# A two-stream, two-layer network on one core: the instruction order drawn up with the tile context's other machine model

## The chip, the core and the metric

One core of one Trainium2 chip runs the whole program in one launch. The metric is the device time of one execution in microseconds; three timed executions of the kernel before gave 1656.62 us as the median (1654.23 to 1677.01). The core's engines are named as in the profile: PE (matrix products; PEld is its weight load), DVE (vector), ACT (scalar), POOL (GpSimd), and SP, which here only issues DMAs. Each engine has its own queue and takes its instructions strictly in the order in which the program lists them; between engines only semaphores hold the order.

## What is computed

Two streams of 128 tokens (a prompt and a sample) with 1024 channels go through two layers. Cut to what matters:

```python
def trunk_layer(x, mod, lp, ...):
    h = adaln(x, norm_g[0], m[0], m[1]);  x = x + 0.5 * m[2] * swiglu(h, ffn_w_in[0], ffn_w_out[0])
    h = adaln(x, norm_g[1], m[3], m[4]);  x = x + m[5] * token_mixing(h)
    h = adaln(x, norm_g[2], m[6], m[7]);  x = x + 0.5 * m[8] * swiglu(h, ffn_w_in[1], ffn_w_out[1])
...
# token_mixing: RWKV, gated linear attention (GLA), gated delta rule and softmax attention beside each other,
# each times a sigmoid gate and a branch matrix, summed, then w_out
```

`m` holds nine modulation vectors of 1024 values per layer, products of the conditioning vector with `w_mod` (1024 x 9216 per layer). RWKV and the delta rule each solve a triangular system of 128 rows per head, direction and stream.

## The kernel before

The tokens of both streams lie together as 256 columns; every large product has a 128x128 block of weights as the stationary operand and 128x256 activations as the moving one. Weights are float32 in HBM. `wload` (L198) loads a block of up to 128x1024 values into a tile `raw` (three buffers) with a DMA of SP's queue (L206). `split` (L177) turns half of it at a time, 512 columns, into two parts `hi` (ACT, L155) and `lo` (DVE, L158), four buffers each; `gemm` (L219) then makes three products for each 128x128 block, `hi` with both parts of the activations and `lo` with the first. So one `lo` row of 128x512 serves 4 x 3 = 12 products, and one full `raw` block 24. All products are issued in `mm`, L170, and are told apart by the tile that they write: `pg`, `pu` and `po` are the gate, up and output products of a feed-forward part (`ffn`, L460) or the gates, branches and output of the mixing; `pA`, `pB`, `pC`, `pD`, `pR`, `pT` are the mixing's input products.

A modulation vector (`mod_part`, L287) needs eight loads of 128x1024 values into tiles `mraw` (L298; 16 buffers) and eight groups of four products `acc` (L170), 64 records in the profile, then a row copy `modrow` and two transposes `acct`. `queue` and `fill` (L325, L338) write these steps in small portions among the products of a feed-forward part: six vectors in the first, four in the second, four in the third, none in the fourth; the loads and products of the last two vectors of each (`KEEP`) are written to fall into the following norm. One more vector per layer is written into the mixing (`queue_mixing`, L1319).

A norm (`rstd`, L380, and `adaln`, L425) ends a sublayer: squares, products `pss`, a chain of eleven small DVE operations on `nr`, products `prs`, then the normalised activations `hhi` and `hlo`, for which the next large product waits.

In the mixing, `ORDER` (L90) lists the steps of a layer with offsets of priority. Both triangular systems go the same way: `gather` (L806) copies 32x32 diagonal blocks from `SA` (RWKV) or `SD` (delta rule) into `GB`, and sends them to DRAM (`d<-GB`); `inverse` (L824) loads them as `Lb<-d` (L834) and inverts all blocks in 31 steps of two POOL operations each (L842 and L843, tiles `itmp` and `Tb`); `inverse_out` (L847) sends the result to DRAM (`d<-Tb`, L852) and back (`TA<-d`, L855), DVE transposes a half of it into `TB` (L857); `solve` (L860) then makes small products `sv` from it, with ACT and DVE steps between them.

The Python code only lists instructions and priorities. The tile context's scheduler plays the program through on a model of the machine and writes each engine's list in the order in which the instructions went there: an instruction that is ready and has the better priority goes first. In what order the engines' lists stand, SP's and POOL's too, follows from that model.

Of the kernel before, what the change touches and what calls it, by code (L numbers as in the profile page):

```python
# [24 lines left out]
OUT_UNITS = ((0, 2), (2, 2), (4, 2), (6, 1), (7, 1))      # first chunk and number of chunks of the output products  # L25
# [4 lines left out]
# column offsets of w_in  # L30
# [3 lines left out]
def constants():  # L34
    """Tables that depend on shapes alone, packed along the free dimension."""
# [28 lines left out]
    for d in range(2):  # L64
        for l in (16, 8, 4, 2, 1):
            tt = (t16 // l) * 2 * l + t16 % l + (l if d == 0 else 0)      # token of a compact index
            su = (si % (2 * l)) >= l
            ms.append(f((si // (2 * l) == tt // (2 * l)) & (su if d else ~su)))
# [33 lines left out]
class Net:  # L102
    def __init__(self, ctx, tc, ia, oa, dbg=None):
# [13 lines left out]
        self.ch = 0                 # which of the two chains of small products is being written  # L117
# [63 lines left out]
    def after(self, later, earlier):  # L181
        """issue order of two instructions of one queue"""
        self.tc.add_manual_dep(later.ins, earlier.ins.name,
                               mybir.DependencyInfo(mybir.DependencyClass.NoSync, mybir.DependencyReason.DATA),
                               reason="issue order")
# [12 lines left out]
    def wload(self, srcs, nk, nc_):  # L198
        """srcs: list of (column offset in tile, dram view [128, nk, n])."""
# [7 lines left out]
        def part(k0, n):  # L207
            """rows k0 .. k0 + n as two f32r parts that sum to them"""
# [10 lines left out]
    def gemm(self, out2, wview, nkc, xhi, xlo, ncol=256, segs=None):  # L219
        """out2: psum tile [128, 512] -> (2, 256) column chunks; weights  # L220
        stationary, channel-major activations moving."""
# [23 lines left out]
    def params_g(self):  # L245
        """conditioning vectors and modulation biases first, the small parameters later"""
# [40 lines left out]
    def mod_part(self, tiles, l, v):  # L287
        """a modulation vector (1024 columns) as loads and products, a pair per weight tile, and a
        last step. Column groups of 256 in the four column tiles of the PE array."""
# [20 lines left out]
        def last():  # L310
# [5 lines left out]
            # chunk of the vector = j * 2 + c  # L316
# [8 lines left out]
    def queue(self, parts):  # L325
        """modulation work for the rest of the sublayer"""
# [11 lines left out]
    def fill(self, nload, nprod):  # L338
        """the queued loads and products up to these counts, the loads never too few"""
# [5 lines left out]
    def flush(self):  # L345
        """what is left, in the shadow of a norm"""
        if self.mr is not None:
            self.fill(len(self.loads), len(self.prods))
            self.mr.close()
            self.mr = None  # L350

    def modcols(self, l, i):
        """per-sublayer columns: g * (1 + scale), shift, gate factor."""
# [13 lines left out]
    def rsqrt(self, p, n, scale, eps):  # L367
        """(p * scale + eps)^-1/2 of [128, n]: a first guess from the exponent, then three
        Newton steps (the sign alternates)"""
# [10 lines left out]
    def rstd(self):  # L380
        """[128, 256] psum: 1 / rms of every token, on all partitions"""
# [21 lines left out]
    def headnorm(self, x, n, scale, eps):  # L403
        """(sum over each 64-partition group of x^2 * scale + eps)^-1/2: psum tiles of 512 columns of x"""
# [20 lines left out]
    def adaln(self, l, i):  # L425
        """x * g (1 + scale) ahead of the norm factor, which comes last; at the start the
        other way round, as the modulation comes last there"""
# [32 lines left out]
    def ffn(self, l, w, i):  # L460
        """the modulation parts are spread over the products; the last steps (keep) wait for the next norm"""
# [39 lines left out]
    # SBUF of this phase is shared by tag: tiles of one tag have disjoint lives.  # L501
# [29 lines left out]
    def padded(self, p):  # L531
        """[128, (2 chunks, 2 streams, 128)] psum -> sbuf with a zero column at each end"""
# [43 lines left out]
    def proj_gate(self, c0, nm):  # L576
        """x * (1 + tanh(x / 2)): silu without its factor 1/2, which is in the norm weights"""
# [8 lines left out]
    def proj_t(self, l):  # L586
        """token-major: values of B and D, the scalar gates of C"""
# [33 lines left out]
    def proj_d(self, l):  # L621
        """q with the heads in the order 0, 2 | 1, 3, and k"""
# [10 lines left out]
    def rwkv_front(self, l):  # L633
# [10 lines left out]
        S0T = self.t("S0T", [128, 4, 128])       # initial state, transposed, block-diagonal over the heads of a chunk  # L644
# [6 lines left out]
        # decay: sg = 2 sigmoid, log-decay = -RW_C * sg  # L651
# [11 lines left out]
        # in-context rates: ta = 2 a - 1  # L663
# [8 lines left out]
        # normalised keys  # L672
        KR = self.t("c4", [128, 2, 2, 256], name="KR")      # stream, chunk, (kk | r)
# [11 lines left out]
        # token-major values  # L685
# [7 lines left out]
        # output gate  # L693
# [11 lines left out]
        # SA: (stream, dir), (L^T | beta.rho^T), head;  UA: right-hand sides, then solutions  # L705
# [6 lines left out]
        for d in range(2):  # L712
# [22 lines left out]
            BK = self.t("e4", [128, 2, 2, 2, 128], name="BK")       # stream, chunk, (beta | kappa)  # L735
# [11 lines left out]
            for s in range(2):  # L747
                sd = 2 * d + s

                def prod(j, e):  # L750
                    """beta or kappa of the heads e, e + 2 against (alpha | rho)"""
# [32 lines left out]
            # final state operands (context only): beta, kappa decayed to the end, token-major  # L784
# [9 lines left out]
        # bonus  # L794
# [11 lines left out]
    def gather(self, S, d):  # L806
        """32x32 diagonal blocks of the systems of a direction to dram, [s', t] for the
        forward direction, transposed for the backward one"""
# [15 lines left out]
    def inverse(self, S, after):  # L824
        """(I + L)^-1 of all 32x32 diagonal blocks by columns; a block's even columns are on
        one partition, its odd ones on another"""
# [33 lines left out]
    def solve(self, S, U):  # L860
        """in place: U <- (I + L)^-1 U by 32-row blocks, both streams of a direction at once"""
# [29 lines left out]
    def state_out(self, p, dst):  # L891
        """the states are the diagonal 64x64 blocks of the two chunks"""
# [4 lines left out]
    def rwkv_back(self, l):  # L897
# [18 lines left out]
        # group norm over each head  # L916
# [15 lines left out]
    def ymix(self, m, y):  # L932
        """y: [128, chunk, stream, tok] -> parts for the branch products"""
# [8 lines left out]
    def delta_front(self, l):  # L942
# [3 lines left out]
        S0 = self.t("S0", [128, 2, 2, 128], name="S0C")     # dir, chunk: [k of two heads, v], block-diagonal  # L946
        nc.sync.dma_start(out=S0, in_=ia["pk_c"][l].rearrange("p (d c v) -> p d c v", d=2, c=2))
        # l2-normalised q (with the 1/sqrt(dk) factor) and k: KQ [stream, chunk, (k | q)]
        big = self.t("big10", [128, 2560], name="delta")
        KQ = big[:, 0:1024].rearrange("p (s c j t) -> p s c j t", s=2, c=2, j=2)  # L950
        EK = big[:, 1024:2048].rearrange("p (d c j t) -> p d c j t", d=2, c=2, j=2)   # dir, chunk, (k | q)
# [6 lines left out]
        # token-major v, and k of the context  # L958
# [11 lines left out]
        # scalars: beta, log-decay  # L970
# [485 lines left out]
```

## Time and profile before

| | |
|---|---|
| median of three timed executions | 1656.62 us (1654.23 to 1677.01) |
| span of the profiled execution, first to last instruction | 1665.8 us |
| time of the profiled execution around its span | not listed; the span stands for it |
| PE busy | 1620.0 us (97%), 13862 matrix instructions |
| DVE, ACT, POOL busy | 1057.8, 811.3, 143.7 us |
| moved by DMA | 311.14 MB, mean 187 GB/s |

The busy time of an engine is the union of its instructions. A product's record lasts longer than the distance to the next one (they are pipelined), so a busy PE need not be at its fastest; distances between starts tell more. A row's releaser in brackets is what ended the engine's idle time just before it.

### The profile page before, as it was taken

How to read it: one execution, taken by the hardware profiler on the slowest of the kernel's cores; microseconds unless marked ns; L12 is line 12 of the kernel's file. 1: busy time of each engine (PE TensorE's matmuls, PEld its weight loads, DVE VectorE, ACT ScalarE, POOL GpSimd, SP SyncE). 2: the span in 40 equal slices, each digit the busy share in tenths (PEclk: the TensorE clock that was granted, in tenths of full speed). 3: DMA queues.
4: the chain of work that ended last, by engine and by line, in shares of the span. 5: the costliest groups of instructions: out<-in, count | busy, mean ns of one | idle time of the engine just before them, and what ended most of it. 6: DMA issues, size and time to landing. Idle time of an engine off the chain costs nothing.

```text
span 1665.8 us, 34996 instructions
## 1 busy us (share of the span) xinstructions
PE 1620.0 (97%) x13862; PEld 1465.2 (88%) x13872; DVE 1057.8 (64%) x2270; ACT 811.3 (49%) x1529; POOL 143.7 (9%) x304
## 2 busy tenths in 40 slices
PE   6999999999999999999999999999999999999997
PEld 3999988788778998999989999887887899989997
DVE  4555557667687477665566655674857774866655
ACT  3444445446444455454455545551744443655553
POOL 0000000043007000000000000000700350000000
PEclk9999999999999999999999999998989998999999
DMA  9998775344246455976669766551423563645553
GB/s 342 315 318 297 238 238 164 80 117 114 64 132 199 127 173 195 324 266 221 213 228 316 245 213 211 189 139 48 122 74 95 158 195 95 187 143 182 186 184 121
DMA packets 300821, 311.14 MB, mean 187 GB/s; under 512 B 48368, under 2 KB 278768, under 8 KB 300656
## 3 DMA queue, kind: packets, MB, share of 16 engines
q1 hardware_dynamic: 300368, 307.85, 58.2%
q8 instruction: 109, 1.79, 0.4%
q10 hardware_dynamic: 288, 1.05, 0.2%
q14 instruction: 56, 0.46, 0.1%
HBM read 303.87 MB, written 4.98 MB: 185 GB/s over the span
## 4 chain that ended last, share of the span: by engine, by line
PE 75%; DVE 4%; POOL 2%; DMA 2%; ACT 2%; issue 1%; SPq 0%; POOLq 0%; DVEq 0%; ACTq 0%
PE pg L170 20%; PE po L170 15%; PE pu L170 13%; PE wk L170 6%; PE sv L170 4%; PE pA L170 3%; PE acc L170 3%; PE pC L170 1%; PE pD L170 1%; PE yA L170 1%; PE pR L170 1%; PE pT L170 1%; POOL itmp L842 1%; POOL Tb L843 1%; DVE lo L158 1%
## 5 line engine op out<-in xcount | busy, mean ns | idle before, releaser
L158 DVE TENSOR_TENSOR lo<-raw,hi 128x512 fp32r<-128x512 f32 (+2 forms) x840 | 581.0, 696 | 394.0 <-ACT hi L155 381.8
L155 ACT ACTIVATE hi<-raw 128x512 fp32r<-128x512 f32 (+2 forms) x840 | 523.2, 626 | 592.4 <-PE pg L170 192.3
L170 PE MATMUL pg<-hhi,hi 128*128 128x256 f32 x1216 | 356.5, 293 | 6.0 <-ACT hi L155 2.9
L170 PE MATMUL pg<-hlo,hi 128*128 128x256 f32 x1216 | 352.8, 290 | 0.5 <-DVE hlo L158 0.3
L170 PE MATMUL pg<-hhi,lo 128*128 128x256 f32 x1216 | 349.7, 288 | 0.8 <-DVE lo L158 0.6
L170 PEld LDWEIGHTS pg<-hhi,hi 128*128 128x128 f32 x1216 | 236.0, 194 | 23.6 <-issue 8.8
L170 PEld LDWEIGHTS pg<-hlo,hi 128*128 128x128 f32 x1216 | 236.1, 194 | 7.7 <-issue 4.4
L170 PEld LDWEIGHTS pg<-hhi,lo 128*128 128x128 f32 x1216 | 236.7, 195 | 3.1 <-DVE lo L158 2.3
L170 PE MATMUL pu<-hhi,lo 128*128 128x256 f32 x704 | 199.3, 283 | 0.0
L170 PE MATMUL pu<-hlo,hi 128*128 128x256 f32 x704 | 199.2, 283 | 0.0
L170 PE MATMUL pu<-hhi,hi 128*128 128x256 f32 x704 | 199.2, 283 | 0.0
L170 PE MATMUL po<-zhi,hi 128*128 128x256 f32 x704 | 198.6, 282 | 0.0
L170 PE MATMUL po<-zhi,lo 128*128 128x256 f32 x704 | 196.8, 280 | 0.0
L170 PE MATMUL po<-zlo,hi 128*128 128x256 f32 x704 | 196.7, 279 | 0.0
L170 PEld LDWEIGHTS po<-zhi,hi 128*128 128x128 f32 x704 | 132.6, 188 | 6.2 <-issue 4.5
L170 PEld LDWEIGHTS pu<-hhi,lo 128*128 128x128 f32 x704 | 135.2, 192 | 0.1
L170 PEld LDWEIGHTS pu<-hhi,hi 128*128 128x128 f32 x704 | 135.2, 192 | 0.0
L170 PEld LDWEIGHTS pu<-hlo,hi 128*128 128x128 f32 x704 | 135.2, 192 | 0.0
L170 PEld LDWEIGHTS po<-zhi,lo 128*128 128x128 f32 x704 | 132.9, 189 | 0.0
L170 PEld LDWEIGHTS po<-zlo,hi 128*128 128x128 f32 x704 | 132.5, 188 | 0.0
L170 PE MATMUL acc<-mraw,cT 128*32 128x256 f32 x1152 | 85.7, 403 | 9.6 <-DMA mraw<-in_w_mod 9.5
L191 POOL COPY GB<-SA 32x128 f32<-32x128 f32 x16 | 5.7, 355 | 911.2 <-DMA out_o_v<-VD 584.6
(354 smaller groups left out, 2610.6 us busy)
## 6 DMA issues: line engine op xcount, KB each, us to landing
raw<-in_ffn_w_in SPq DMA_DIRECT2D x176, 512.0 KB, 4.5
mraw<-in_w_mod SPq DMA_DIRECT2D x138, 512.0 KB, 5.7
raw<-in_w_in SPq DMA_DIRECT2D x106, 512.0 KB, 3.6
raw<-in_ffn_w_out SPq DMA_DIRECT2D x76, 512.0 KB, 4.4
raw<-in_w_branch SPq DMA_DIRECT2D x32, 256.0 KB, 3.2
raw<-in_w_out SPq DMA_DIRECT2D x16, 512.0 KB, 4.1
raw<-in_ffn_w_out SPq DMA_DIRECT2D x12, 256.0 KB, 3.0
raw<-in_ffn_w_out SPq DMA_DIRECT2D x8, 384.0 KB, 4.4
```

Of the source, the lines that this page charges most:

```text
L155: self.nc.scalar.activation(out, in_, func, bias=bias, scale=scale, **kw)
L158: self.nc.vector.tensor_tensor(out, a, b, op)
L170: self.nc.tensor.matmul(out, lhsT, rhs, start=start, stop=stop)
L191: (self.nc.vector if eng == "v" else self.nc.gpsimd).tensor_copy(out, in_)
L842: nc.gpsimd.tensor_tensor(tv, a, b, ALU.mult)
L843: nc.gpsimd.tensor_tensor(T[:, 0:n, j + 1:32], T[:, 0:n, j + 1:32], tv, ALU.subtract)
```

## The change

The scheduler is told to use its other model of the machine, a simulation of the timeline, when it draws up the order. No instruction is added, removed or altered; matched by name, both programs hold the same 11988 products, 701 DMAs on SP, 2270 DVE and 1508 ACT operations. Waits on semaphores follow the new order. The rest of the diff removes comments.

```diff
-    with _tile.TileContext(nc, pool_alloc_mode="queue") as tc:
+    with _tile.TileContext(nc, pool_alloc_mode="queue", schedule_with_timeline_sim=True) as tc:
         build(tc, ia, oa)
```

First place: SP's queue at the start of the first feed-forward part. Before, from the first three weight blocks on:

```order
L206 DMA raw<-in_ffn_w_in 128x4x256 x3
L298 DMA mraw<-in_w_mod 128x1024 x2
L206 DMA raw<-in_ffn_w_in 128x4x256
L298 DMA mraw<-in_w_mod 128x1024
L253 DMA cst<-in_consts 128x1348
L206 DMA raw<-in_ffn_w_in 128x4x256 x3
L254 DMA wg<-in_constb 128x2688
L206 DMA raw<-in_ffn_w_in 128x4x256
L298 DMA mraw<-in_w_mod 128x1024 x4
L206 DMA raw<-in_ffn_w_in 128x4x256 x3
```

Now, from the same three blocks on:

```order
L206 DMA raw<-in_ffn_w_in 128x4x256 x3
L253 DMA cst<-in_consts 128x1348
L254 DMA wg<-in_constb 128x2688
L298 DMA mraw<-in_w_mod 128x1024 x7
L206 DMA raw<-in_ffn_w_in 128x4x256
L298 DMA mraw<-in_w_mod 128x1024
L206 DMA raw<-in_ffn_w_in 128x4x256
L298 DMA mraw<-in_w_mod 128x1024 x8
L206 DMA raw<-in_ffn_w_in 128x4x256
L298 DMA mraw<-in_w_mod 128x1024 x7
```

This goes on until all 48 `mraw` loads of the six vectors are issued, with 8 weight blocks among them; 33 weight blocks without a modulation load follow. PE's list has moved in the same way: all six vectors' `acc` products stand before the second half of the sixth of 22 `pg` and `pu` groups. In the second feed-forward part the list has the loads of eight vectors, its own four and the four of the third part, 64 `mraw` with 15 weight blocks among them, behind the part's first five blocks and before its last 24 (`ffn_w_in`); their `acc` products stand in the first ten of its 22 groups. The third part has none left.

Second place: PE at the norm after the first feed-forward part. Before:

```order
L170 MATMUL po<-zhi,lo 128x256
L170 MATMUL acc<-mraw,cT 32x256 x8
L170 MATMUL pss<-ones,ssq 128x1 x4
L170 MATMUL pss<-ones,sq 128x1 x2
L170 MATMUL acc<-mraw,cT 32x256 x5
L170 MATMUL pss<-ones,sq 128x1 x2
L170 MATMUL acc<-mraw,cT 32x256 x16
L170 MATMUL prs<-cst,nr 128x128 x2
L170 MATMUL acc<-mraw,cT 32x256 x3
L175 MATMUL acct<-cst,modrow 128x128 x2
L170 MATMUL acc<-mraw,cT 32x256 x32
L170 MATMUL pA<-hhi,hi 128x256
```

Now:

```order
L170 MATMUL po<-zhi,lo 128x256
L170 MATMUL pss<-ones,ssq 128x1 x4
L170 MATMUL pss<-ones,sq 128x1 x4
L170 MATMUL prs<-cst,nr 128x128 x2
L170 MATMUL pA<-hhi,hi 128x256
```

The `acc` products are gone from this norm, and in the same way from the four other norms that lie between sublayers.

Third place: SP's queue around the inversion for RWKV in the first layer (`Lb` is POOL's input, `d<-Tb` its result; the second layer has the same rows). Before:

```order
L834 DMA Lb<-d_3700 64x1024 x2
L206 DMA raw<-in_w_in 128x4x256 x7
L1220 DMA out_o_k<-QD 128x128
L206 DMA raw<-in_w_in 128x4x256
L852 DMA d_4706<-Tb 1024x1x32 x2
L206 DMA raw<-in_w_in 128x4x256
L855 DMA TA<-d_4706 128x16x32
```

Now:

```order
L834 DMA Lb<-d_3700 64x1024 x2
L206 DMA raw<-in_w_branch 128x2x256
L206 DMA raw<-in_w_in 128x4x256
L1220 DMA out_o_k<-QD 128x128
L852 DMA d_4706<-Tb 1024x1x32 x2
L855 DMA TA<-d_4706 128x16x32
```

Of eight weight blocks of 512 KB between POOL's input and its result, one is left, with one block of 256 KB. On DVE, 23 `lo` operations of 128x512 stood between the last `GB<-SA` and `TB<-TA`, now 5 do; for the delta rule 32 stood between the last `GB<-SD` and its `TB<-TA`, now 21. Both counts are the same in the second layer. For the delta rule, the first `sv` products on PE now stand behind the gate products that were interleaved with the solution before; a stretch of PE's list there, now:

```order
L170 MATMUL pg<-hhi,lo 128x256
L170 MATMUL sv<-UD,SD 96x64 x8
L170 MATMUL sv<-UD,SD 32x64 x8
L170 MATMUL sv<-UD,TA 32x64 x8
L170 MATMUL sv<-UD,TB 32x64 x8
L170 MATMUL sv<-UD,SD 64x64 x8
L170 MATMUL sv<-UD,SD 32x64 x8
L170 MATMUL sv<-UD,TA 32x64 x8
L170 MATMUL sv<-UD,TB 32x64 x8
L170 MATMUL sv<-UD,SD 32x64 x16
```

Before, three to twelve `pg` products stood behind each such pair of rows; now the solution runs to its end without one.

## Rows read from the trace of the kernel before

**Rows 1.** The page's head and part 1: busy time and share of each engine.

```profile
span 1665.8 us, 34996 instructions
PE 1620.0 (97%) x13862; PEld 1465.2 (88%) x13872; DVE 1057.8 (64%) x2270; ACT 811.3 (49%) x1529; POOL 143.7 (9%) x304
```

**Rows 2.** Windows: stretch, length, busy of PE, PEld, DVE, ACT, POOL, clock, DMA, GB/s.

```profile
10.00:20.00 10.00, 8.59 (x56) 5.13 (x50) 1.78 (x11) 0.00 (x0) 0.00 (x0) 1.00 1.03 410
30.00:60.00 30.00, 28.58 (x212) 26.15 (x212) 20.03 (x44) 17.81 (x37) 0.00 (x0) 0.89 0.92 324
0.00:1665.00 1665.00, 1619.97 (x13862) 1465.18 (x13872) 1057.79 (x2270) 811.34 (x1529) 143.75 (x304) 0.98 0.59 187
```

**Rows 3.** The chain that ended last, by time: start, length, what.

```profile
1477.23 5.76 PE pg L170 x48
```

**Rows 4.** Timeline of PE: first gate product, first products of both solutions.

```profile
30.96 0.39 PE L170 MATMUL pg<-hhi,hi 128*128 128x256 f32 x1 [1.97 <-ACT hi L155]
...
401.88 0.91 PE L170 MATMUL sv<-UA,TA 32*32 32x64 f32 x13
...
551.43 0.91 PE L170 MATMUL sv<-UD,TA 32*32 32x64 f32 x13
```

**Rows 5.** Timeline of PE, norms after the first and the second feed-forward part.

```profile
248.78 0.28 PE L170 MATMUL po<-zhi,lo 128*128 128x256 f32 x1
...
258.58 3.66 PE L170 MATMUL acc<-mraw,cT 128*32 128x256 f32 x64
262.17 0.39 PE L170 MATMUL pA<-hhi,hi 128*128 128x256 f32 x1
...
843.30 0.28 PE L170 MATMUL po<-zhi,lo 128*128 128x256 f32 x1
...
855.47 0.39 PE L170 MATMUL pg<-hhi,hi 128*128 128x256 f32 x1
```

**Rows 6.** Timeline of PE after an idle time in the first feed-forward part.

```profile
240.10 0.69 PE L175 MATMUL acct<-cst,modrow 128*128 128x128 f32 x2 [3.21 <-ACT modrow L155]
...
240.81 0.41 PE L170 MATMUL po<-zhi,hi 128*128 128x256 f32 x1
...
242.72 0.41 PE L170 MATMUL po<-zhi,hi 128*128 128x256 f32 x1
```

**Rows 7.** Timeline of PE: end of a norm, and the last norm (no `acc`).

```profile
638.13 0.71 PE L170 MATMUL prs<-cst,nr 128*128 128x128 f32 x4 [0.35 <-DVE nr L161]
...
640.47 0.39 PE L170 MATMUL pg<-hhi,hi 128*128 128x256 f32 x1
...
1654.34 0.28 PE L170 MATMUL po<-zhi,lo 128*128 128x256 f32 x1
...
1658.59 0.71 PE L170 MATMUL prs<-cst,nr 128*128 128x128 f32 x4 [2.22 <-DVE nr L161]
```

**Rows 8.** Timeline of SP's queue, first RWKV inversion: start, length, row.

```profile
347.25 1.16 SPq L834 DMA_DIRECT2D Lb<-d  x2
...
389.41 1.28 SPq L852 DMA_DIRECT2D d<-Tb  x2
```

**Rows 9.** Timeline of DVE: last RWKV gather, first results of both inversions.

```profile
343.49 1.24 DVE L818 STREAM_TRANSPOSE GB<-SA 32x128 f32<-32x128 f32 x4
...
397.46 0.45 DVE L857 STREAM_TRANSPOSE TB<-TA 128x256 f32<-128x256 f32 x1 [2.05 <-DMA TA<-d]
...
547.14 0.44 DVE L857 STREAM_TRANSPOSE TB<-TA 128x256 f32<-128x256 f32 x1
```

**Rows 10.** Timeline of POOL, first RWKV inversion: first, two middle, last.

```profile
351.96 0.24 POOL L842 TENSOR_TENSOR itmp<-Lb,Tb 128x31 f32<-128x31 f32 x1 [22.36 <-DMA Lb<-d]
...
361.81 0.74 POOL L842 TENSOR_TENSOR itmp<-Lb,Tb 128x126 f32<-128x126 f32 x1
...
372.76 0.43 POOL L842 TENSOR_TENSOR itmp<-Lb,Tb 128x126 f32<-128x126 f32 x1
...
389.15 0.24 POOL L843 TENSOR_TENSOR Tb<-Tb,itmp 128x16 f32<-128x16 f32 x1
```

## The prediction, written before the changed kernel ran

> **What bounds the kernel now.** I read the page's shares first, then windows, then the chain that ended last, then the timelines of single engines at the places where the order moves. The page has PE busy for 1620.0 of 1665.8 us [rows 1]: only 45.8 us of the span are without a product. Over the whole run the granted clock is 0.98 and the DMA engines are at work 59% of the time [rows 2]. The chain agrees: in its last part it runs along PE's own products, at an even pitch, 48 in 5.76 us or 0.12 us each [rows 3]. So PE's throughput is the bound almost everywhere, and the loads, DVE and POOL are covered. All 11988 products remain and each takes what it took; a new order of them can therefore gain no more than the idle time and the little that the clock lost, while it can lose wherever PE runs out of work that is ready. The question is where the cover that the old order gave to transfers and chains is gone. I count from the profile's span, 1665.8 us. No time around it is listed; it stands 9.2 us above the median of the runs, 1656.6, so 9 are taken off at the end.
>
> **Loads in the first feed-forward part.** Now all 48 modulation loads of 512 KB come before the ninth weight block behind the first three. PE starts its first gate product at 30.96 us [rows 4]. A stretch with modulation loads alone moves 410 GB/s, so 512 KB (524 KB in thousands) take 1.28 us; the mixed stretch from 30 to 60 us moves 324, which is 1.62 us [rows 2]. 48 x 1.28 + 8 x 1.62 = 74.4 us. In this time PE can do 11 blocks of 24 products at 0.12 (31.7 us) and six vectors at 3.66 us [rows 5], 22.0, together 53.7. It must wait 20.7 us. One loss of the old order goes: an idle time of 3.21 us late in this part, and behind it twelve products at 0.21 instead of 0.12 us [rows 6], together 4.3. I take **+16**. Ends: 5 if seven of the loads have landed before 30.96, 33 if all 56 blocks go at 1.62. Behind the late `mraw` on PE's list stand the gate products, whose blocks lie behind the same loads in SP's queue; nothing there can run ahead.
>
> **Loads in the second part.** 64 loads stand among the first twenty weight blocks. I let five of them land during the norm, into free buffers: 59 x 1.28 + 15 x 1.62 = 99.8 us, and 2.9 until the first block is free (24 x 0.12). PE has 20 x 24 x 0.12 = 57.6 and eight vectors at 3.66, 29.3, so 86.9. **+16**. Ends: 8 with eleven loads landed before, 36 with all at 1.62. The third part has then no vector; its own weights, one block per 2.9 us of products against 1.6 us of transfer, are no bound.
>
> **Norms.** The filled norm after the first part takes 13.39 us from its last `po` to the first `pA` and has two vectors in it, 7.3 us of products that must be done somewhere [rows 5]: it costs 6.1 itself; the one after the second part, also with two vectors, takes 12.17 and costs 4.9 [rows 5]. I take 5.0 for the mean of the five. Without filler the time from the last `po` to `prs` is 4.25, and 2.34 more pass from `prs` to the next large product [rows 7]: 6.6. With PE idle for some 4 us of it I add 1.1 for a clock that comes back late [rows 6]. 7.7 less 5.0 is 2.7, five times: **+14**. Ends: 3 where the old norms ran at a lowered clock anyway, 25 where the whole idle time of 4 us and the clock come on top.
>
> **Inversion for RWKV.** The chain is fixed: last gather at 343.49, `Lb` issued at 347.25, POOL from 351.96 to 389.39, `d<-Tb` at 389.41, `TB<-TA` at 397.46 [rows 8 to 10], first `sv` on PE at 401.88 [rows 4]. PE was busy beside it; 4.4 us lay between `TB` and `sv`, in which the chain could have been longer. Between the gather and `TB` 18 fewer `lo` are on DVE's list, and each feeds twelve products: 18 x 12 x 0.12 = 25.9 us of cover gone, less the 4.4, about 22 in each of two layers: **+44**. DVE's queue waits in the `TB` operation, with all later `lo` behind it; SP waits in `d<-Tb` for POOL, with the next weight blocks behind it, so PE gets nothing else, and when the result is there the loads start cold. Ends: 12 and 31 a layer. The lower is for a shorter POOL: the same operation of 128x126 takes 0.74 us in one place and 0.43 in another [rows 10], and 28 of the 62 operations were like the first; at 0.31 less each POOL ends 9 us earlier. The upper adds the cold start.
> The Trainium skill, page "SBUF — State Buffer", section "Who interferes with whom", says that a DVE instruction with two inputs in SBUF contends with a GpSimd instruction that reads SBUF, since they share one pair of ports. `lo<-raw,hi` is such an instruction, and the trace with its two durations agrees. By that page fewer `lo` would make POOL faster, 44 would become 26 and the sum 18 less. I don't take it whole, because the stretch still has other two-input operations.
>
> **Inversion and solution of the delta rule.** 11 fewer `lo`: 15.8 us of cover, less the slack from `TB` at 547.14 to `sv` at 551.43 [rows 4, 9], 4.3: 12 a layer, **+24** (ends 8 and 20 a layer). The solution loses its gate products; its small products wait for ACT and DVE steps. I give it 6 us a layer, **+12**, by the nearest row, the unfilled norm of 6.6 us [rows 7], with ends 0 and 10 a layer. After four long waits the clock comes back late, 1.1 each: **+5** (0 to 8).
>
> **Sum.** 16 + 16 + 14 + 44 + 24 + 12 + 5 = 131. 1665.8 + 131 = 1797 in a profile; less 9, **1788 us**.
>
> **Rivals.** (a) The order helps after all: not slower. Its place is the mixing. If PE reaches the first `sv` only after `TB`, because PE's own small products stretch over the whole chain, the inversions cost nothing, and the products moved behind the solutions fill what was idle there. All idle time is 45.8 us [rows 1] and the lost clock 2% of 1666, 33 us [rows 2]; with half of both regained the mixing would give back about 39, and if the loads cost only 13 and the norms 3, the run would take some 1634. It decides from the point at which five `lo` and the small products last for 54 us. Against it: in the old order the five, the 18 and the small products together lasted just so long. Chance 0.03.
> (b) The bursts go at the mixed rate of 324 GB/s: 33 + 36 in place of 32, so +37: 1825. For it: ACT and DVE splits and other loads lie beside these, as in the mixed stretch. Against it: the rate there may be what PE asked for. Chance 0.13.
> (c) The inversions wait no longer than before, because the work missing between gather and result stands between result and `sv` on PE's list: without 44, 24 and 5 it is +58: 1715. For it: products whose `lo` was made before the gather can still be to do, up to four `lo` tiles in their buffers. Against it: four tiles are 48 products, 5.8 us of the 25.9, and the old order had such tiles too. Chance 0.09.
> That the scheduler's switch does nothing is out: the lists differ.
>
> **How the numbers follow.** The forecast has 0.75. The range reaches from (c) to beyond (b): **1715 to 1860**, which also holds the sums with two of the large terms at either end together. A change of 2%, 1623 to 1690, is about what a measurement of this kernel can tell from no change. Slower needs +33, which the loads and the norms almost give by themselves: faster 0.02, same 0.04, slower 0.94.
>
> **What would show it.** Right: in the first 40 us of the first two feed-forward parts PE idle behind `mraw` loads at about 400 GB/s, and the third part at an even pitch with no `acc`; five norms with 4 to 5 us idle; DVE's `TB<-TA` in RWKV ending a wait of over 15 us on `TA`, with PE idle before `sv`; about 10 us of that for the delta rule. Wrong: POOL done in 28 us and PE busy until `sv` (then the inversions are not the cost); a rate near 324 (then the loads cost double); or PE's pitch above 0.12 in stretches without gaps, which no term here has.

## The result, and the profile after

The changed kernel takes **1836.05 us** (1833.87 to 1840.37, four runs) against 1661.26 us of the kernel before in the same series: 1.104 times the time, interval 1.096 to 1.111. That is 175 us more; the forecast was 131 more, 1788 us, in a range of 1715 to 1860. The span of the profiled execution is 169.7 us longer than that of the one before.

The page's head and part 1 after the change, which answer to [rows 1]:

```profile
span 1835.5 us, 35025 instructions
PE 1674.9 (91%) x13872; PEld 1515.6 (83%) x13872; DVE 1053.5 (57%) x2270; ACT 816.4 (44%) x1529; POOL 126.3 (7%) x304
```

PE is idle for 160.6 us (1835.5 - 1674.9) where it was for 45.8, so 115 us of the 170 are waiting. But PE is also *busy* for 55 us more with the same products: busy time grew without work, while the mean granted clock fell from 0.979 to 0.919. The rows below show where products ran slower.

The places come next. For each part of the program I took the time from one start to the next in PE's timeline: from the last `po` before a norm to the first large product behind it (a norm), and from there to the next last `po` (a sublayer); the opening counts from PE's first product, at 8.2 and 8.3 us, and the 11.5 us behind the last `po`, the same in both, are left out. Since `acc` products moved between parts, they are taken out at 0.0572 us a record (3.66 us for 64, [rows 5]); the last columns are what the part costs beyond them.

| part | before, us | after, us | `acc` records before, after | cost | forecast |
|---|---|---|---|---|---|
| opening and first feed-forward part | 240.6 | 261.6 | 384, 512 | 13.8 | 16 |
| second feed-forward part, and third | 403.6 | 445.2 | 256, 512 | 26.9 | 16 |
| five norms, and the fourth part behind the last | 244.2 | 228.4 | 508, 0 | 13.3 | 14 |
| first mixing | 370.3 | 440.1 | 2, 64 | 66.3 | 42.5 |
| second mixing | 387.5 | 440.4 | 2, 64 | 49.4 | 42.5 |

The costs add up to 169.7. Two rows came out near the forecast; the second feed-forward part and the mixings did not.

Windows of the changed kernel, columns as in [rows 2]: the burst of loads in the second feed-forward part, then five stretches of the first mixing: gather to first `sv` of RWKV, its solution, gather to first `sv` of the delta rule, its solution, and the rest up to the norm.

```profile
729.86:842.18 112.32, 102.86 (x983) 75.21 (x981) 34.71 (x68) 28.24 (x52) 0.00 (x0) 0.95 1.00 376
396.00:443.30 47.30, 24.92 (x154) 19.51 (x153) 21.74 (x51) 17.49 (x40) 26.23 (x65) 0.68 0.25 56
443.30:486.60 43.30, 43.30 (x420) 37.20 (x421) 19.30 (x52) 15.43 (x28) 0.00 (x0) 0.80 0.21 62
577.50:630.00 52.50, 38.42 (x321) 36.96 (x313) 26.16 (x47) 16.88 (x28) 31.40 (x62) 0.92 0.53 136
630.00:659.30 29.30, 25.58 (x227) 23.58 (x227) 6.74 (x11) 5.34 (x9) 0.00 (x0) 0.50 0.13 40
659.30:717.30 58.00, 55.22 (x438) 50.87 (x437) 35.84 (x82) 27.87 (x51) 0.00 (x0) 0.86 0.44 133
```

The same view of the kernel before: gather to `sv` and solution of RWKV, gather to `sv` and solution of the delta rule, all in the first layer, and both solutions in the second.

```profile
344.40:401.90 57.50, 56.31 (x441) 50.31 (x439) 44.31 (x91) 36.83 (x81) 33.42 (x65) 1.00 0.49 137
401.90:424.50 22.60, 22.24 (x307) 18.41 (x309) 14.30 (x45) 9.55 (x18) 0.00 (x0) 1.00 0.17 49
491.00:551.40 60.40, 57.36 (x484) 54.46 (x483) 42.17 (x81) 26.98 (x48) 31.68 (x62) 0.97 0.69 197
551.40:575.30 23.90, 23.90 (x291) 22.20 (x291) 10.05 (x15) 8.22 (x14) 0.00 (x0) 0.93 0.30 89
1216.60:1245.30 28.70, 28.18 (x306) 23.00 (x309) 13.46 (x43) 9.64 (x18) 0.00 (x0) 0.76 0.11 36
1370.00:1398.70 28.70, 28.44 (x292) 26.35 (x291) 10.84 (x17) 9.13 (x16) 0.00 (x0) 0.76 0.28 82
```

The start of that burst on SP's queue, and the part's first product on PE:

```profile
729.86 2.41 SPq L298 DMA_DIRECT2D mraw<-in_w_mod  x5
```

```profile
724.04 0.58 PE L170 MATMUL pg<-hhi,hi 128*128 128x256 f32 x1 [1.24 <-ACT hhi L155]
```

In the windows, read length minus PE's busy time first: 47.30 - 24.92 = 22.4 us idle before the RWKV solution (1.2 before), 14.1 before the delta rule's (3.0 before). Then the clock. The delta rule's solution now runs at 0.50 from end to end, that is at the lower of the two levels, 1.2 GHz, and takes 29.3 us with three large products in it; before, it held 67 large ones and took 23.9. And the kernel before shows what the clock alone does: its two layers have the same list, but RWKV's solution takes 22.6 us at a clock of 1.00 in the first and 28.7 at 0.76 in the second. Why the clock fell in the second, where PE had been busy for all but 1.9 of the 59 us before, no row shows.

RWKV's solution in the changed kernel shows how the clock comes back. Its first 14.8 us, and the `pg` products on PE that follow:

```profile
443.30:458.10 14.80, 14.80 (x101) 11.77 (x102) 2.79 (x5) 3.98 (x7) 0.00 (x0) 0.50 0.12 35
```

```profile
458.76 0.41 PE L170 MATMUL pg<-hhi,hi 128*128 128x256 f32 x1
458.98 0.41 PE L170 MATMUL pg<-hlo,hi 128*128 128x256 f32 x1
...
460.82 0.28 PE L170 MATMUL pg<-hlo,hi 128*128 128x256 f32 x1
460.94 0.28 PE L170 MATMUL pg<-hhi,lo 128*128 128x256 f32 x1
```

No large product lies in the first 14.8 us. PE is busy throughout, and the clock stays at 0.50. Then large products come at a pitch of 0.21 us, and after ten of them at 0.12; the rest of the solution runs at 1.00.

The chain of the inversion, which answers to [rows 4, 8, 9, 10]. SP's queue:

```profile
398.93 1.68 SPq L834 DMA_DIRECT2D Lb<-d  x2
400.70 0.54 SPq L206 DMA_DIRECT2D raw<-in_w_branch  x1
407.48 0.37 SPq L206 DMA_DIRECT2D raw<-in_w_in  x1
...
436.20 1.28 SPq L852 DMA_DIRECT2D d<-Tb  x2
```

POOL, first and last instruction of the inversion and two of its operations of 128x126:

```profile
405.94 0.24 POOL L842 TENSOR_TENSOR itmp<-Lb,Tb 128x31 f32<-128x31 f32 x1 [34.00 <-DMA Lb<-d]
...
416.11 0.74 POOL L842 TENSOR_TENSOR itmp<-Lb,Tb 128x126 f32<-128x126 f32 x1
416.93 0.44 POOL L843 TENSOR_TENSOR Tb<-Tb,itmp 128x126 f32<-128x126 f32 x1
...
435.94 0.23 POOL L843 TENSOR_TENSOR Tb<-Tb,itmp 128x16 f32<-128x16 f32 x1
```

PE, the two waits for the result, and a norm without `acc` (which answers to [rows 5]):

```profile
443.29 0.52 PE L170 MATMUL sv<-UA,TA 32*32 32x64 f32 x3 [7.41 <-DMA TA<-d]
...
630.03 1.27 PE L170 MATMUL sv<-UD,TA 32*32 32x64 f32 x10 [10.38 <-DMA TA<-d]
...
976.67 0.28 PE L170 MATMUL po<-zhi,lo 128*128 128x256 f32 x1
...
983.87 0.58 PE L170 MATMUL pg<-hhi,hi 128*128 128x256 f32 x1 [1.24 <-ACT hhi L155]
```

One weight block of 512 KB is issued between `Lb` and `d<-Tb` where there were eight. POOL needs 30.2 us (405.94 to 436.17) where it needed 37.4, and still PE waits: its last idle time before `sv` is 7.41 us, and most of the rest of the 22.4 lies in two earlier waits of 7.0 and 6.1 us between the small products beside the inversion. The norm takes 983.87 - 976.67 = 7.20 us with nothing in it but itself.

### The profile page after: what moved, and what is told of

Read it like the earlier page. It is cut to its first block, busy times and chain, and to the rows that moved or that the text cites. A ratio compares the mean times of both kernels' runs of the same rounds, so it can differ in the third digit from the quotient of the medians.

```text
span 1835.5 us, 35025 instructions
## 1 busy us (share of the span) xinstructions
PE 1674.9 (91%) x13872; PEld 1515.6 (83%) x13872; DVE 1053.5 (57%) x2270; ACT 816.4 (44%) x1529; POOL 126.3 (7%) x304
## 4 chain that ended last, share of the span: by engine, by line
PE 74%; DMA 13%; POOL 6%; DVE 4%; issue 2%; ACT 1%; SPq 1%; DVEq 0%; POOLq 0%; ACTq 0%
PE pg L170 20%; PE po L170 16%; PE pu L170 14%; DMA raw<-in_ffn_w_in 5%; PE wk L170 5%; PE sv L170 5%; DMA mraw<-in_w_mod 4%; PE pA L170 3%; POOL Tb L843 3%; POOL itmp L842 3%; PE pC L170 2%; PE pR L170 1%; DMA Lb<-d 1%; PE pD L170 1%; PE pT L170 1%
## 5 line engine op out<-in xcount | busy, mean ns | idle before, releaser
L170 PE MATMUL pg<-hhi,lo 128*128 128x256 f32 x1216 | 356.8, 293 | 1.3 <-DVE lo L158 1.1
L170 PEld LDWEIGHTS pg<-hhi,hi 128*128 128x128 f32 x1216 | 243.5, 200 | 22.1 <-ACT hi L155 9.4
L170 PEld LDWEIGHTS pg<-hhi,lo 128*128 128x128 f32 x1216 | 242.7, 200 | 9.7 <-issue 5.1
L170 PEld LDWEIGHTS pg<-hlo,hi 128*128 128x128 f32 x1216 | 243.1, 200 | 8.7 <-DVE hlo L161 5.5
L170 PEld LDWEIGHTS acc<-mraw,cT 128*32 128x32 f32 x1152 | 32.2, 115 | 51.4 <-DMA mraw<-in_w_mod 20.8
```

Of the source, the lines that this page charges most:

```text
L170: self.nc.tensor.matmul(out, lhsT, rhs, start=start, stop=stop)
```

## The experiments

Five kernels start from the changed one: four give a part back and one adds products. Five start from the kernel before, keep the scheduler's old model and take over a part of the new order. They pin the order of issue: `after(later, earlier)` (L181) tells the scheduler to put one instruction behind another. `raws` is a list of the DMAs of all weight blocks, `mods` one of all modulation loads, and `hold[n]` names what the n-th weight block is put behind. The diffs are cut to the pins. Ratios are to the kernel before in the same series; there it took 1676 us in the median in two series and 1666 in the third, against 1661 beside the changed kernel, so kernels of different series are better compared by their ratios, which are good to about 1%. Lengths of solutions and mixings are from the profiles.

**Giving back the paced loads.** Each modulation load stands behind the weight block that is written before it:

```diff
-                self.nc.sync.dma_start(out=t, in_=w[:, k, c0:c0 + n])
+                d = self.nc.sync.dma_start(out=t, in_=w[:, k, c0:c0 + n])
+                if self.raws:
+                    self.after(d, self.raws[-1])
```

> The changed kernel, but each modulation load is pinned in SP's queue behind the weight block written before it, so that the bursts of mraw loads are gone; three of the five norms get their acc products back, the inversions keep the new order. Theory (of the 175 us about 11 to 14 come from the burst in the first feed-forward part, 27 from that in the second, 10 from the norms, the rest from the mixing): 1790 us (1780 to 1800), the second feed-forward part back near 203 us with half the vectors, both mixings still 440 us. Rival (the second part is long because PE comes out of the mixing at a low clock, and the loads are hidden anyway): 1820 or more.

Measured: 1806.75 us, ratio 1.083 (1.074 to 1.092). The second feed-forward part is back at 205.8 us (252.6 in the changed kernel), the first, counted from its first gate product, at 214.7 (236.4); three norms are filled again and take 11.4 to 11.7 us; the two mixings are 446.8 and 445.8 us. The rival is out: this part lay in the loads. The total is 7 us above the upper end, but the series was a slower one (by the ratio it is 35 us less than the changed kernel); the mixings, which the theory had as unchanged, are some 6 us longer each.

**Giving back the cover of the inversions.** The eighth last block of the projections goes behind RWKV's `Lb`, a block of the gates and branches behind the delta rule's:

```diff
+        if after == TAILA:
+            self.after(self.raws[-8], lb)
+        else:
+            self.hold[self.nraw + 17] = [lb]
```

> The changed kernel, but the weight block that followed the inversion's input in the old order is pinned in SP's queue behind that input, for RWKV and for the delta rule, so that large products lie beside both inversions and both solutions again; the bursts of loads and the empty norms stay. Theory (the waits before sv and the slow clock that follows them make about 115 of the 175 us): mixings of 370 to 390 us instead of 440, 1720 us (1705 to 1740), idle of PE before sv under 6 us. Rival (only the waits go, 64 us, and the solutions stay slow because their small products are slow in the new order whatever lies before them): 1770.

Measured: 1812.21 us, ratio 1.086 (1.077 to 1.095), mixings of 426.5 and 426.4 us. Both expectations fail. 20 and 26 `lo` stand beside the inversions now, but PE still waits for 11 and 6 us there, and only one solution is fast, the one that has no wait right in front of it and many large products in it. Its windows: RWKV's solution (22 large products) and the delta rule's (156):

```profile
435.50:476.70 41.20, 40.50 (x303) 33.95 (x304) 14.42 (x32) 12.12 (x26) 0.00 (x0) 0.53 0.14 41
614.50:647.60 33.10, 33.10 (x381) 31.47 (x380) 16.41 (x25) 14.44 (x24) 0.00 (x0) 1.00 0.44 127
```

RWKV's takes 41.2 us at 0.53, behind a wait of 6.2 us; the one in the kernel before, with the same `sv` products but partly other small ones beside them, took 22.6 at 1.00. The delta rule's has 156 x 0.12 = 18.7 us of large products in its 33.1, so its 223 small ones cost 14.4 us; in the changed kernel they cost 28.9.

**Both together.**

> Both pins together. Theory (the two parts add up): 1675 us (1655 to 1700), what is left being two unfilled norms and the rest of the order. Rival (the new order loses time in many small places besides these): over 1720.

Measured: 1779.79 us, ratio 1.067 (1.056 to 1.078). The two gains add up (29 and 24 us alone, 56 together; by the ratios 0.021, 0.018 and 0.037), but what is left is over 100 us, and the rival is right in number. Both mixings are still 431 us: the wait before RWKV's `sv` is there (6.9 and 5.9 us in the two layers), and so is the slow solution.

**More cover.** The pins of the kernel above, but `raws[-13]` and `self.nraw + 14`:

> The kernel with both pins (paced loads, covered inversions), the pinned weight blocks five earlier for RWKV and three earlier for the delta rule: 24 and 31 lo beside the inversions, and 87 large products inside the RWKV solution in place of 15. In the kernel with both pins the RWKV solution ran at a granted clock of 0.50 to 0.55 behind a wait of 6 us. Theory (the low clock behind a wait is what is left): no wait over 3 us before sv, the solution's clock over 0.8 and its length about 30 us for five times the large products, each mixing about 402 us in place of 431, 1722 us (1705 to 1740). Rival (the new order is slow in itself): 1765 or more.

Measured: 1753.30 us, ratio 1.055 (1.042 to 1.068), between the two. The solution of RWKV in the first layer of the kernel with both pins, and then in this one (39.0 us at 0.54 and 34.7 at 0.95 in the second):

```profile
421.50:460.00 38.50, 37.78 (x296) 31.30 (x297) 13.33 (x30) 13.10 (x32) 0.00 (x0) 0.55 0.06 18
```

```profile
418.30:453.30 35.00, 34.95 (x374) 30.05 (x375) 17.87 (x38) 16.59 (x36) 0.00 (x0) 0.94 0.26 77
```

With 87 large products in place of 15 the solution is 4 us *shorter*: 35.0 - 72 x 0.12 = 26.4 us for what took 38.5, at a clock of 0.94 after 0.55. That part of the theory holds. Two things changed at once, though: there are more large products, and the wait right in front of the solution is gone. This run does not tell them apart. But the mixings are 421 and 419 us, not 402: the blocks that now lie beside the chain are missing ahead of the gather, where this kernel idles for 10.5 us.

**Filling the wait.** 56 products without use on PE's list just before the first RWKV `sv`, in the kernel with both pins:

```diff
             p = self.wkt("sv")
+            for k in range(WARM if S is self.SA and d == 0 and rows.start == 0 else 0):
+                self.after(self.nc.tensor.matmul(p[:, 0:256], self.h[0][:, 0, 0:128],
+                                                 self.h[0][:, k % 8, :], start=True, stop=True), self.ta)
```

> The kernel with both pins, with 56 additional products of 128x256 (hhi by hhi, written to the solution's tile and then overwritten) on PE's list just before the first RWKV sv of each layer, in the wait of 6 us; they add nothing that is used. Theory (PE's idle time there lowers the clock, and the low clock makes the solution slow): the solution's clock near 1, its length 38 us down to about 27 with its 45 more large products, 1779 down to 1755 although work is added. Rival (the solution is slow because of its ACT and DVE steps): the solution stays at 38 to 44 us, 1780 to 1790.

Measured: 1789.35 us, ratio 1.078 (1.069 to 1.087); the solution takes 47.6 us at 0.59. It does not test the theory, because the wait was not filled. PE's timeline there:

```profile
412.82 3.64 PE L880 MATMUL sv<-hhi 128*128 128x256 f32 x29
422.67 1.08 PE L177 MATMUL wk<-cst,Pm 128*128 128x128 f32 x4 [6.21 <-DVE Pm L160]
```

The scheduler put most of the products ahead of a step of the attention whose input comes from DVE behind the same late `TB`; the wait moved in front of that step, with 6.21 us as before. Still it says one thing. This solution holds 60 large products where the kernel with both pins has 15, behind a like wait, and it is no shorter: 47.6 us at 0.59, and 42.4 at 0.69 in the second layer, against 38.5 and 39.0. More large products in a solution did not make up for the wait in front of it.

**The old scheduler with the bursts.** From the kernel before: each of 23 weight blocks goes behind the modulation load that it stands behind in the changed kernel's list.

```diff
+        for r, m in EARLY.items():
+            net.after(net.raws[r], net.mods[m])
```

> The kernel before with its own scheduler's model, but the weight blocks of the first two feed-forward parts are pinned behind the same modulation loads as in the changed kernel; three norms lose their acc products with it, the mixing keeps the old order. Theory (the bursts cost by themselves): 1706 us (1695 to 1720), the first part longer by about 11 us beyond its additional products, the second by 28. Rival (the bursts cost only what the new order of PE around them costs): under 1680.

Measured: 1718.51 us, ratio 1.029 (1.020 to 1.038): in the expected range, at its upper end. The second feed-forward part takes 253.0 us (252.6 in the changed kernel), the first 238.7, three unfilled norms 7.2 us each; the mixings stay. Its burst, in a window:

```profile
662.00:775.00 113.00, 99.75 (x975) 75.15 (x974) 37.11 (x77) 29.50 (x57) 0.00 (x0) 0.95 0.99 373
```

113 us with the DMA engines at 0.99 and 373 GB/s: the bursts cost the same whichever model made the rest of the order.

**The old scheduler with bare inversions.** RWKV's last gather goes behind an `lo`, and a later block behind `TA`:

```diff
+        for gb, r, a, ta in net.late:
+            if a == TAILA:
+                net.after(gb, net.los[r + 2])
+                net.after(net.raws[r + 6], ta)
```

> The kernel before with its own scheduler's model, but the last gather for RWKV is pinned behind the lo operations of the third weight block after the projections, and the blocks from three further on behind the result's load TA: 5 lo stand beside the RWKV inversion in place of 23, and 22 beside that of the delta rule in place of 32, as in the changed kernel. Norms and modulation loads keep the old order. Theory (the waits before sv and the low clock behind them cost by themselves): PE idle 20 us before the first RWKV sv and 10 before that of the delta rule, the RWKV solution over 35 us, each mixing 30 to 45 us longer than before, 1740 us (1725 to 1755). Rival (what is taken out of the wait fills other gaps, and the rest of the new order is what costs): under 1700.

Measured: 1750.83 us, ratio 1.052 (1.042 to 1.062). PE idles for 20.3 us before RWKV's `sv` and 17.8 before that of the delta rule, the RWKV solution takes 33.7 us (expected: over 35), the mixings 415.4 and 416.3 us, 45 and 29 more than in the profile of before. Gather to `sv`, solution, and the delta rule's gather to `sv` and solution:

```profile
397.00:443.40 46.40, 26.06 (x231) 19.05 (x231) 21.54 (x75) 12.12 (x27) 25.56 (x65) 0.81 0.22 52
443.40:477.10 33.70, 33.70 (x335) 31.55 (x335) 13.26 (x20) 12.42 (x21) 0.00 (x0) 0.81 0.37 112
533.80:590.60 56.80, 38.97 (x302) 37.30 (x300) 28.16 (x54) 16.96 (x29) 28.42 (x62) 0.82 0.53 138
590.60:614.50 23.90, 23.90 (x292) 22.19 (x291) 10.06 (x16) 8.28 (x14) 0.00 (x0) 0.93 0.28 82
```

The delta rule's wait does not end at its `sv` here but at large products:

```profile
583.47 0.58 PE L171 MATMUL pg<-hhi,hi 128*128 128x256 f32 x1 [17.78 <-ACT hi L156]
```

Behind it stand 36 large products, the first 24 mostly at a pitch of 0.21 us, the last ones at 0.12, and then the solution, which takes 23.9 us at 0.93, the same as in the kernel before. So a wait of 17.8 us cost the solution nothing where large products stood between the two.

**The old scheduler with a late inversion.** Only `Lb` is pinned, behind the block that it follows in the changed kernel:

```diff
+        for lb, r in net.late:
+            net.after(lb, net.raws[r])
```

> The kernel before with its own scheduler's model, but the inversions' inputs Lb are pinned behind the same weight blocks as in the changed kernel, 13 blocks later for RWKV, without any pin on what follows; 39 lo stand then beside the RWKV inversion. Theory (it is the missing cover that costs, not the later start): within 15 us of the kernel before. Rival (the later start costs, because the solution and all behind it come later): 1690 or more.

Measured: 1775.42 us, ratio 1.070 (1.060 to 1.080). The theory missed by over 80 us and the rival is right. I had counted 39 `lo` between gather and `TB`, but most of them are done before `Lb`: SP issues 14 weight blocks between the gather at 342 us and `Lb` at 400.19, and four between `Lb` and `d<-Tb`. RWKV's window from `Lb` to the first `sv`, and the solution behind it:

```profile
400.20:446.80 46.60, 32.31 (x278) 24.86 (x279) 26.64 (x81) 16.33 (x34) 28.34 (x65) 0.87 0.36 89
446.80:482.00 35.20, 35.16 (x340) 33.29 (x341) 12.72 (x20) 11.35 (x19) 0.00 (x0) 0.78 0.31 94
```

PE idles for 14.3 us there. It idles for 20.3 us before the delta rule's `sv` too (3.0 in the kernel before), although 34 `lo` stand beside that inversion. So in this run the later start took the cover away: a block that is done before the chain starts is not there when the chain runs.

**The old scheduler with a bare solution.** The weight blocks behind the delta rule's inversion go behind the state that its solution writes:

```diff
+        for r, e in zip(net.outs[1::2], net.ends[3::4]):
+            net.after(net.raws[r + 0], e)
```

> The kernel before with its own scheduler's model, but the two weight blocks that went between the delta rule's inversion and its solution, and all later ones, are pinned behind the solution's state output: no large product stands in the solution (67 before), 29 lo beside the inversion in place of 32. Theory (a solution alone on PE falls to the lower clock and so does the head output behind it; the term of 6 us a layer was too small): the solution at a clock near 0.5 and over 27 us with no large product in place of 24 with 67, that is 11 us or more a layer net, some 6 more behind it, 1700 us (1690 to 1715). Rival (6 us a layer, as forecast): 1670 to 1680.

Measured: 1691.64 us, ratio 1.018 (1.011 to 1.026), some 30 us by the ratio (18 to 43), where the forecast had 12 in all. The profiles put it on one layer: the mixings take 395.7 and 386.9 us, where the kernel before has 370.3 and 387.5, and its second was at a low clock in places already. The solution of both layers, with no large product in it:

```profile
550.10:576.10 26.00, 23.08 (x254) 20.34 (x254) 4.38 (x7) 4.11 (x7) 0.00 (x0) 0.62 0.00 1
1373.90:1396.70 22.80, 19.86 (x254) 17.40 (x254) 4.92 (x8) 4.11 (x7) 0.00 (x0) 0.76 0.01 1
```

The clock falls, but not at once to 0.50, and the solution stays under the 27 us that I expected. One difference lies at its start: here PE comes to it busy, in the changed kernel out of a wait of 10 us.

**The old scheduler with all of these** (bursts, bare inversions, bare solution):

> The kernel before with its own scheduler's model and all pins of old_with_bursts, old_bare_inversions and old_bare_solution at once: the modulation loads early, five norms empty, 5 and 19 lo beside the inversions (5 and 21 in the changed kernel), no large product in the delta rule's solution. Theory (these four things are the whole change): 1830 us (1810 to 1850), each stage within some 8 us of the changed kernel. Rival (the new order loses elsewhere too): under 1800.

Measured: 1843.80 us, ratio 1.108 (1.100 to 1.115); the changed kernel has 1.104. The parts agree as well: second feed-forward part 253.4 us (252.6), mixings 438.0 and 438.7 (440.1 and 440.4), all norms 7.2 to 7.4. Inside the mixing they agree less: RWKV's solution is 33.3 us (43.3), but fewer large products lie in it (111 in place of 115) and fewer small ones. The two gathers to `sv` and the two solutions in the first layer:

```profile
421.00:467.30 46.30, 26.21 (x233) 19.06 (x231) 21.52 (x75) 12.12 (x27) 25.53 (x65) 0.83 0.23 51
467.30:500.60 33.30, 33.27 (x334) 31.18 (x335) 13.27 (x20) 12.26 (x21) 0.00 (x0) 0.82 0.38 114
557.40:607.30 49.90, 31.58 (x267) 30.45 (x266) 24.08 (x47) 13.10 (x22) 28.99 (x62) 0.84 0.43 111
607.30:638.50 31.20, 28.28 (x254) 24.03 (x254) 4.90 (x8) 4.11 (x7) 0.00 (x0) 0.50 0.00 1
```

The bare solution is at 0.50 again, now that it comes straight out of a wait, 18.3 us long. The three single ratios add up to 9.9% and all together give 10.8; the difference lies within the intervals, so the parts are independent as far as these runs can tell. These four things (bursts, empty norms, bare inversions, a bare solution) are enough to make the old order as slow as the new one. Taking them out of the new order was done only in part, and gave back only a part.

## Why the prediction was right, and where it was not

**That it gets slower, and where: right.** PE's throughput was the bound, no product became cheaper, and each of the named places cost time: the old order with just these things in it takes the time of the new one. The forecast was still 44 us short.

**Idle time of the mixing: right to a few us.** From the windows, before RWKV's `sv` 22.4 and 22.1 us in the two layers against 1.2 and 1.9: 41 (forecast 44). Before that of the delta rule 14.1 and 14.2 against 3.0 and 1.9: 23 (24). In its solution and behind it 14.0 against 0.6 for both layers: 13 (12). Together 78, where the forecast had 80.
The 44 was right by two errors that offset each other. PE's list lost more cover than the 18 `lo` said: 262 large products fewer between gather and `sv`, 31 us at 0.12, not 25.9. And POOL took 30.2 us in place of 37.4. The Trainium skill, page "SBUF — State Buffer", section "Who interferes with whom", has it that a DVE instruction with two inputs in SBUF contends with a GpSimd instruction that reads SBUF; I had weighed this and not taken it. The trace agrees with it: operations of 128x126 take 0.74 us at one place and 0.43 or 0.44 at others [rows 10 and above], and with fewer `lo` beside them fewer of the inversion's 62 operations are long, 9 over 0.55 us where there were 28.

**The clock: the step that failed.** I had written: "After four long waits the clock comes back late, 1.1 each: +5". The mixings cost 116 us, 78 of them idle, so 38 are products that ran slower. The 1.1 us came from [rows 6], where large products follow the wait and the clock is back after twelve of them. Behind these waits stand solutions of small products, and there the clock did not come back after 1.1 us: RWKV's solution now runs at 0.80, at 0.50 for its first 14.8 us, the delta rule's at 0.50 for all of its 29.3 us, the end of the mixing at 0.86 [windows above]. What ended the low clock in RWKV's solution was a run of large products, as in [rows 6]; behind the wait of 17.8 us in the old order with bare inversions it was the same, and the solution behind those products lost nothing. The number of large products strewn over a solution does not decide it: 60 of them came to 0.59 and 0.69 behind a wait, 115 to 0.80, 87 without a wait to 0.94. My list of signs of being wrong had "PE's pitch above 0.12 in stretches without gaps, which no term here has"; RWKV's solution has no gap and a pitch of 0.21. That a solution can run slow was in the trace of before: the same solution of 22.6 us in one layer took 28.7 in the other, at 0.76, and I read only the first.

**The second burst: mis-sized, 27 in place of 16.** Two assumptions: I let five loads land during the norm, but none goes out before 729.86 us, 5.8 us after the part's first product. I let the modulation loads go at 410 GB/s, the rate of a stretch of 10 us; the burst of 112 us moves 376, with the DMA engines at 1.00. That is 1.39 us for a load of 512 KB rather than 1.28. The rival with 324 GB/s (1.62 us) was wrong, but the truth lay a third of the way to it. How the 11 us divide between the two was not measured. The first burst, priced with the same two rates, came to 13.8 with the opening (16).

**Norms: right**, 13.3 for 14, of which 2.9 is in the fourth part's beginning: 7.2 or 6.8 us each, the forecast 6.6 and a late clock.

**The rivals.** The helpful one is out: idle time in the mixings grew from 15 to 93 us. The third, no longer waits, is out by the same rows.

**The range** held because the ends were taken from bounds on each term; the upper end of the clock term, 8, was wrong by 30, and the other ends covered it. That the time fell inside is in part luck: the range had no room meant for slow products.

What stays open: the kernel with more cover kept 51 and 31 us over the kernel before in its two mixings, part of it ahead of the gather. How much of that is cover moved from one place to the other and how much the finer order of the small products was not taken apart. A wait before RWKV's `sv` filled on purpose was not measured either; only the row with large products behind the delta rule's wait bears on it.

## What to carry to other kernels

Independent work beside a serial chain is a stock that can be spent once: when a reordering runs it earlier, count what is left for the chain *while it runs*, from the issue of its input to its result, and for the small products behind it too. Where an engine's clock depends on what it does, an idle time costs itself and, if small products follow, up to the length of these once more (14.4 us at a clock of 1.00 and 28.9 at 0.50 for the delta rule's here); look for the same instructions at two clocks in the trace of before, and price the loss from there. A rate for a long burst is read from a long stretch.

## What the runs showed that I had not expected

PE can be busy for 25.6 of 29.3 us with small products and stay at a clock of 0.50 all that time, and for the whole of 14.8 us in RWKV's solution. The same bare solution ran at 0.62 and 0.76 when PE came to it busy, and at 0.50 out of a wait. And a stretch can get shorter although work is added: 35.0 us with 87 large products and no wait in front, 38.5 with 15 behind a wait. Large products alone do not hold the clock: with 67 of them and no wait in front, the delta rule's solution in the kernel before ran at 0.93 in one layer and 0.76 in the other.
